# Two gate blocks by seven products of halves, and their layer's gate modulation moved to a later stage

## The chip, the cores and the metric

The kernel runs on one core of a Trainium2 chip. The metric is the device time of one execution in microseconds, as the median of several runs. The engines are TensorE (PE, its weight loads are listed as PEld), VectorE (DVE), ScalarE (ACT), GpSimd (POOL) and SyncE (SP). SP does no arithmetic here; it issues nearly all loads. POOL issues the stores to DRAM scratch.

## The reference

A trunk of two layers on 512 tokens of width 2048. Layer 1 is multi-scale retention, layer 2 multi-head latent attention with 16 heads. Each layer also has a SiLU gate path, and a modulation by a conditioning vector `c`:

```python
c_act = jax.nn.silu(c)
for i in range(DEPTH):
    mod = (c_act @ ada_w[i] + ada_b[i])[:, None, :]
    shift, scale, gate = jnp.split(mod, 3, axis=-1)
    h = rmsnorm(x, norm_g[i]) * (1.0 + scale) + shift
    y = branch(h)
    x = x + gate * y
return rmsnorm(x, final_norm_g)
```

and in the attention branch:

```python
proj = h @ w_in
cq, ckv, k_rope, g = jnp.split(proj, [512, 1024, 1088], axis=-1)
q = rmsnorm(cq, q_norm_g) @ w_uq
kv = rmsnorm(ckv, kv_norm_g) @ w_ukv
o = causal_block_attention(q, k, v)
return (jax.nn.silu(g) * o) @ w_out
```

The change concerns two things of layer 2: columns 1024 to 2047 of `g` (the third and fourth block of 512), and the third section of `mod`, the vector `gate` of 2048 values, which is first needed when the output projection is added to the residual.

## The kernel before

**Numbers.** Every operand of a large product is split in two parts: `hi` is the value rounded to the matmul's 32-bit type (ACT casts it), `lo` the rest (DVE subtracts). A product is three matmuls, hi·hi, hi·lo and lo·hi (`mm3`, lines 160 to 163). The activations of layer 2, `h2`, lie in SBUF as 16 tiles of 128 rows by 512 tokens in both parts.

**Two ways to multiply.** `plain_steps` (L727) walks through eight units of two 128-row tiles; a unit is 24 matmuls of 128x512 (two tiles, four column blocks, three parts). The other way halves both the columns of the weights and the tokens, and forms seven products of halves instead of eight, as in Strassen's scheme with Winograd's sums. It needs sums of halves of the activations, formed once (`form_sums`, L447, 16 tiles of `sums2` for layer 2), and sums of halves of the weights, formed by DVE for each unit. `seven_steps` (L795) does so for products whose result has tokens on its rows, among them the latents `cq` and `ckv`. `seven_rows_steps` (L876) does it for products with tokens along the free axis; layer 1's `q` and `k` of four heads use it. A block is eight steps: in the first phase four units of four products (48 matmuls of 128x256), in the second four units of three products (36 matmuls). Its four accumulators x, s, z, y are four PSUM banks of the tag `acc`.

**Order of layer 2.** The main loop takes a list of `steps`, each with its loads, a preparation (splits and sums of weights), its matmuls and what is hung beside it. Gate block 0 and 1 come first, then the latents, then gate blocks 2 and 3 (the list `g23`, 16 steps by `g2_steps`, L1613), and nine attention steps (`attention_step`, L1983), each of which projects two heads and attends the two before. The Silu of each gate block is stored in DRAM (`sg2_d`) and read back per head (`sg`). While `g23` runs, the latents are normed, transposed on PE and split into `k4` tiles. The last two heads are attended in hooks of the output projection, which has two runs of eight units (`o2_unit`, 24 matmuls of 128x512 each) and a last part of its own. `o2_parts` loads the attention's result (`o_in`) and splits it into `o_h` and `o_l`; `o2_unit` loads and splits `o_w`. In `o2_out` (L2192 to 2210) the gate vector multiplies the result.

**The gate's modulation.** `later_modulation` (L1061) loads the modulation's rows in pieces of 512 KB (`mod`) and DVE sums each against `silu(c)` with one instruction (L1078). The pieces of layer 2's gate, 32 of them, are requested by the argument `rows=2` of the 16 steps of `g23`: two loads a step, each summed one step later. Their buffers are `bw` (two) and `pt` (four); `silu(c)` lies in two `k4b` tiles.

**Order on the engines.** The program is emitted through a scheduler that may reorder instructions on an engine by their priority. `behind(engines)` holds what follows behind the last instruction already emitted on those engines; `queued(fn)` does so for ACT, DVE, PE and SP. Each engine then runs its instructions strictly in the resulting order, and a waiting instruction holds up everything behind it. Buffers are rings: a tile of a tag with two buffers waits until the last user of the tile before the last is done.

**Buffers of the sums.** `sums_tile(n)` (L443) puts sums tiles 0 to 7 into the eight `k4` buffers, 8 to 11 into `k4b`, 12 to 15 into `pt`. Unit `u` of the scheme reads tile `2u` in its first phase (`i = 0`) and `2u + 1` in its second.

Of the kernel before, what the change touches and what calls it, by code (L numbers as in the profile page):

```python
# [9 lines left out]
F32 = mybir.dt.float32  # L10
# [39 lines left out]
def hybrid_trunk_kernel(  # L50
# [44 lines left out]
    def big(name, dt=F32R):  # L95
        return base.tile([P, 2, T], dt, tag="big", bufs=16, name=name)
# [7 lines left out]
    def tmp(name, shape=(P, T)):  # L104
        return base.tile(list(shape), F32, tag="tmp", bufs=6, name=name)
# [325 lines left out]
    def queued(fn, *args):  # L431
        with behind(A_, V_, T_, S_):
            return fn(*args)
# [5 lines left out]
    def sums_tile(n, more):  # L439
        shape = [P, 2, 2, H]  # L440
        if n < 8:
            return base.tile(shape, F32R, tag="k4", bufs=8, name=f"sums_{n}")
        if n < 12:  # L443
            return base.tile(shape, F32R, tag="k4b", bufs=4, name=f"sums_{n}")
        return more(shape, f"sums_{n}")

    def form_sums(u, acts, sums, staged, more, late=False):  # L447
        e, o = (tmp(f"h_{2 * u + i}_f") for i in range(2))
        for f, kt in ((e, 2 * u), (o, 2 * u + 1)):
            DVE.tensor_add(f, acts[kt][:, 0, :].bitcast(F32), acts[kt][:, 1, :].bitcast(F32))  # L450
        f = staged(f"sums_{u}_f")
        DVE.tensor_add(f[0][:, 0, :], e[:, H:], o[:, H:])
        DVE.tensor_sub(f[0][:, 1, :], f[0][:, 0, :], e[:, :H])
        DVE.tensor_sub(f[1][:, 0, :], e[:, :H], e[:, H:])
        DVE.tensor_sub(f[1][:, 1, :], o[:, :H], f[0][:, 1, :])

        def part():
            for i in range(2):
                s = sums[2 * u + i] = sums_tile(2 * u + i, more)
                split(f[i], s[:, :, 0, :], s[:, :, 1, :])  # L460

        if late:
            return part
        part()
# [1148 lines left out]
    def g2_steps(gi, **kw):  # L1613
        def evac(b, ps):
            sgs = l2_tile("sg", 3, f"sgs_{gi}_{b}")
            ACT.activation(sgs, ps, AF.Silu)
            r0 = (gi * 4 + b) * P
            POOL.dma_start(sg2_d[r0 : r0 + P, :], sgs)

        return plain_steps(  # L1620
            8, 2, lambda u: [(whole, rows(w_mla_in, u, 2, 1088 + gi * 512, 512))], 512, f"g2_{gi}", acc, 4,
            lambda w, ki, kt, b: w_block(w, ki, b), lambda w, ki, kt, b: act_row(h2[kt]), evac, **kw,
        )
# [91 lines left out]
        return l2_tile("pt", 4, name, shape, F32R)  # L1715

    for u, step in enumerate((ga[5], ga[7], g1[0], g1[2], g1[3], g1[5], g1[6], g1[7])):
        step.beside["form"].append(lambda u=u: form_sums(u, h2, sums2, staged2, more2))

    latent = {}  # L1720

# [12 lines left out]
    def latent_norm(n):  # L1734
        if n == "q":
            DVE.tensor_scalar(out=qn_s, in0=qn_c, scalar1=192.0**-0.5, scalar2=None, op0=ALU.mult)
        ss = small(f"ss_{n}", NT)
        for t in range(NT):
            ACT.activation(tmp(f"{n}_sq{t}"), latent[n][t], AF.Square, accum_out=ss[:, t : t + 1])
        latent[n, "r"] = rsqrt(ss, NT, 1.0 / 512, f"{n}_r")  # L1740

    def latent_scale(n):
        for t in range(NT):
            r, v = latent[n, "r"][:, t : t + 1], latent[n][t]
            if t % 2:
                ACT.activation(v, v, AF.Identity, scale=r)
            else:
                DVE.tensor_scalar(out=v, in0=v, scalar1=r, scalar2=None, op0=ALU.mult)

    def latent_transposes(n):  # L1750
        latent[n, "ps"] = []
        for j in range(4):
            ps = aux(f"{n}T_{j}")
            for t in range(NT):
                PE.transpose(ps[:, t * P : (t + 1) * P], latent[n][t][:, j * P : (j + 1) * P], ident)
            latent[n, "ps"].append(ps)

    def latent_parts(n, g_c):
        latent[n, "T"] = []
        for j, ps in enumerate(latent[n, "ps"]):  # L1760
            dst = k4(f"{n}T_{j}")
            ACT.activation(dst[:, 0, :], ps, AF.Identity, scale=g_c[:, j : j + 1])
            DVE.scalar_tensor_tensor(
                out=dst[:, 1, :], in0=ps, scalar=g_c[:, j : j + 1], in1=dst[:, 0, :].bitcast(F32),
                op0=ALU.mult, op1=ALU.subtract,
            )
            latent[n, "T"].append(dst)
# [7 lines left out]
        "c", lambda kt, j: wc[kt * P : (kt + 1) * P, j, :], lambda n, u, b: form(h2, sums2, n, u, b), *turns2,  # L1775
        latent_rows, lambda second, u: 0,
    )
    g23 = g2_steps(2, rows=lambda u: 2) + g2_steps(3, rows=lambda u: 2)
    for i, n, g_c in ((0, "q", qn_s), (1, "kv", kvn_c)):
        g23[i].beside["form"].append(lambda n=n: latent_norm(n))  # L1780
        g23[i + 1].beside["form"].append(lambda n=n: latent_scale(n))
        g23[2 + 2 * i].beside["multiply"].append(lambda n=n: latent_transposes(n))
        g23[3 + 2 * i].beside["form"].append(lambda n=n, g_c=g_c: latent_parts(n, g_c))
    steps += g23


# [69 lines left out]
    def units_ahead():  # L1856
        with behind(S_):
            while unit_state[0] < min(unit_state[1] + 3, len(unit_order)):
                unit_load(*unit_order[unit_state[0]])
                unit_state[0] += 1  # L1860
# [46 lines left out]
    def attend(h):  # L1907
# [72 lines left out]

        return scores, exps, lambda: (queued(reciprocals), queued(normalise)), transposes, split_pt, load_gate, values, result

    def attention_step(pr):  # L1983

        nx = pr + 1
        here = [attend(2 * pr + s) for s in range(2)] if pr >= 0 else ()
        both = heads2[nx] = {}
        units_ahead()
        if here:
            (sc0, ex0, no0, tr0, sp0, lg0, va0, re0), (sc1, ex1, no1, tr1, sp1, lg1, va1, re1) = here  # L1990
            queued(lg0)
            queued(lg1)
        low = next_unit("ukv")
        if here:
            for i in range(NT):
                queued(sc0, i)
            for i in range(NT):
                queued(ex0, i)
        low()
        if here:  # L2000
            no0()
        queued(uq_products, nx, 2)
        if here:
            for i in range(NT):
                queued(sc1, i)
            for i in range(NT):
                queued(ex1, i)
        t1 = queued(rope_own, both["uq", 2], f"qr_{nx}")
        low = next_unit("ukv") if here else lambda: None
        if here:  # L2010
            no1()
        low()
        for b in range(2):
            queued(uq_products, nx, b)
        sw = queued(rope_swap, both["uq", 2], f"qr_{nx}")
        low = queued(part_pair, nx, "uq", 0)
        queued(rope_turn, t1, sw)
        queued(low)
        low = queued(part_pair, nx, "uq", 1)
        if here:  # L2020
            queued(tr0)
        queued(low)
        lows = [queued(sp0, j) for j in range(3)] if here else []
        both["qr"] = big(f"qr_{nx}")
        queued(rope_highs, t1, both["qr"])
        for low in lows:
            queued(low)
        queued(rope_lows, t1, both["qr"])
        for b in range(2):
            queued(uk_products, nx, b)  # L2030
            low = queued(part_pair, nx, "uk", b)
            low_w = next_unit("uq")
            queued(low)
            low_w()
        if here:
            queued(va0)
            queued(re0)
            queued(tr1)
            for low in [queued(sp1, j) for j in range(3)]:
                queued(low)  # L2040
        for j in range(2):
            queued(uv_products, nx, j)
            queued(queued(part_values, nx, j))
        if here:
            queued(va1)
            queued(re1)
# [12 lines left out]
    def all_rows():  # L2059
        pieces = [(0, 2, 0), (0, 2, 1), (1, 0, 0)]  # L2060
        yield from later_modulation(pieces, load_c(lpp, "bm", 2), lpp, [("bw", 2)])
        while "l1" not in pools:
            yield None
        l1p = pools["l1"]
        pieces = [(1, 0, 1), (1, 1, 0), (1, 1, 1)]
        yield from later_modulation(pieces, load_c(l1p, "odd1", 2), l1p, [("odd0", 2)])
        while "l2" not in pools:
            yield None
        yield from later_modulation(
            [(1, 2, n) for n in range(2)], load_c(base, "k4b", 4), pools["l2"], [("bw", 2), ("pt", 4), ("pt", 4)]  # L2070
        )

    later = all_rows()
    loads = [load for step in steps for load, _ in step.units]
# [93 lines left out]
    ss2 = l2p.tile([P, T], F32, tag="o2", bufs=2, name="x2_ss")  # L2168
    o2_in, o2_res = {}, {}

    def o2_hooks(i):
        l2_hooks.get(i, lambda: None)()

    def o2_parts(r, u):
        if u not in o2_in:
# [223 lines left out]
```

## Time and profile before

| | us |
|---|---|
| median of 3 runs | 2168.11 (2167.63 to 2168.21) |
| the profiled execution | 2168.69 |
| its span in the trace | 2166.9 |

The span in layer 2, read from the trace:

| stage | from, us | to, us |
|---|---|---|
| gate block 1 | 1475 | 1554 |
| latents by seven products | 1554 | 1631 |
| gate blocks 2 and 3, plain | 1631 | 1722 |
| attention steps | 1722 | 1963 |
| last heads and the projection's first two runs | 1963 | 2050 |
| last part of the projection and the end | 2050 | 2167 |

Gate block 1's row includes the forming of sums and the rotary key beside it. A row of a timeline gives start, duration, engine, line, operation, destination and sources, and in brackets how long the engine stood idle before it and what ended that. "MATMUL ... x48" is a group; a matmul's duration is longer than the distance of two starts, since they are pipelined. A row of stretches gives start and end, length, and for each engine its busy time with the number of instructions in brackets, then the granted clock of TensorE, the share of the DMA engines and GB/s.

### The profile page before, as it was taken

The numbers are of one execution on the slowest core, as the hardware profiler recorded it, in microseconds if no ns is written. First come the engines' busy times: TensorE is split into PE (matmuls) and PEld (weight loads), VectorE is DVE, ScalarE is ACT, GpSimd is POOL, SyncE is SP. The second block draws the span as 40 slices with busy tenths as digits, with TensorE's granted clock in tenths as the row PEclk, the third lists the DMA queues.
The fourth block names the chain that finished last, engine by engine and source line by source line (L and its number), as shares of the span: only waits on it lengthen the run. The fifth ranks groups of instructions, "written<-read, shape, count | busy, mean of one in ns | idle before, by whom it ended". The sixth has DMA issues, their size and how long they took to land.

```text
span 2166.9 us, 29190 instructions
## 1 busy us (share of the span) xinstructions
PE 2138.3 (99%) x10796; PEld 1817.2 (84%) x10796; DVE 1637.7 (76%) x2426; ACT 1038.9 (48%) x1580; POOL 106.1 (5%) x178
## 2 busy tenths in 40 slices
PE   8899999999999999999999999999999999999998
PEld 6788898988889888888888888888888889888887
DVE  7898788788878789766777777667977677775545
ACT  5674444444444444434344444445444365664444
POOL 1001000000000000000000000010001000000000
PEclk9999999999999999999999999999999999999999
DMA  9975687877777778765646557553458623335333
GB/s 382 381 282 192 222 272 233 270 243 257 260 255 252 231 238 280 246 200 173 231 163 224 203 201 251 173 177 103 161 185 319 244 88 100 92 106 183 111 101 136
DMA packets 218753, 456.08 MB, mean 210 GB/s; under 512 B 20161, under 2 KB 69345, under 8 KB 214769
## 3 DMA queue, kind: packets, MB, share of 16 engines
q1 hardware_dynamic: 206400, 415.04, 57.2%
q0 software_dynamic: 11920, 38.91, 4.6%
q8 instruction: 84, 1.38, 0.3%
q14 instruction: 59, 0.48, 0.1%
q10 hardware_dynamic: 290, 0.27, 0.1%
HBM read 411.15 MB, written 43.00 MB: 210 GB/s over the span
## 4 chain that ended last, share of the span: by engine, by line
PE 85%; DVE 5%; issue 4%; DMA 3%; ACT 2%; POOL 1%; SPq 0%; POOLq 0%; DVEq 0%; ACTq 0%
PE o L1376 12%; PE o L2235 4%; PE y L796 2%; PE y L797 2%; PE s L796 2%; PE y L795 2%; PE s L797 2%; PE x L797 2%; PE x L796 2%; PE s L795 2%; PE x L795 2%; PE x_qk L894 2%; PE y_qk L894 2%; PE s_qk L894 2%; PE o L162 2%
## 5 line engine op out<-in xcount | busy, mean ns | idle before, releaser
L1376 PE MATMUL o<-o_h,o_whi 128*128 128x512 f32 (+1 forms) x496 | 192.3, 388 | 0.0
L1376 PE MATMUL o<-o_h,o_wlo 128*128 128x512 f32 (+1 forms) x496 | 191.5, 386 | 0.1
L1376 PE MATMUL o<-o_l,o_whi 128*128 128x512 f32 (+1 forms) x496 | 191.3, 386 | 0.0
L1376 PEld LDWEIGHTS o<-o_h,o_wlo 128*128 128x128 f32 x496 | 93.2, 188 | 19.3 <-DVE o_wlo L136 0.6
L1376 PEld LDWEIGHTS o<-o_l,o_whi 128*128 128x128 f32 x496 | 93.2, 188 | 18.3
L1376 PEld LDWEIGHTS o<-o_h,o_whi 128*128 128x128 f32 x496 | 93.2, 188 | 18.3
L136 DVE TENSOR_TENSOR o_wlo<-o_r,o_whi 128x1024 fp32r<-128x1024 f32 x61 | 74.6, 1224 | 44.2 <-ACT o_whi L135 44.2
L161 PE MATMUL g<-h,g_h 128*128 128x512 f32 x232 | 90.6, 391 | 0.3 <-ACT g_h L135 0.3
L162 PE MATMUL g<-h,g_h 128*128 128x512 f32 x232 | 90.3, 389 | 0.0
L163 PE MATMUL g<-h,g_l 128*128 128x512 f32 x232 | 89.8, 389 | 0.0
L161 PE MATMUL qk<-hT,qk_h 128*128 128x512 f32 x192 | 74.9, 390 | 0.0
L162 PE MATMUL qk<-hT,qk_h 128*128 128x512 f32 x192 | 74.7, 389 | 0.0
L356 DVE SCALAR_TENSOR_TENSOR aw<-aw,c_all 128x2048 f32<-128x2048 f32 (+1 forms) x35 | 72.9, 2103 | 0.9 <-DMA aw<-in_ada_t_dram 0.9
L135 ACT CAST o_whi<-o_r 128x1024 fp32r<-128x1024 f32 x61 | 63.5, 1051 | 21.0 <-PE o L1376 17.6
L163 PE MATMUL qk<-hT,qk_l 128*128 128x512 f32 x192 | 73.4, 389 | 0.0
L1078 DVE SCALAR_TENSOR_TENSOR mod<-mod,c_odd 128x1024 f32<-128x1024 f32 x48 | 58.1, 1221 | 18.5 <-DMA mod<-in_ada_t_dram 18.5
L136 DVE TENSOR_TENSOR o_w_lo<-o_w_raw,o_w_hi 128x1024 fp32r<-128x1024 f32 x32 | 39.0, 1221 | 36.7 <-ACT o_w_hi L135 36.7
L136 DVE TENSOR_TENSOR o_l<-o_in,o_h 128x1024 fp32r<-128x1024 f32 x24 | 29.3, 1223 | 42.8 <-ACT o_h L135 42.8
L1078 DVE SCALAR_TENSOR_TENSOR mod<-mod,c_bm 128x1024 f32<-128x1024 f32 x48 | 58.6, 1220 | 0.0
L2235 PE MATMUL o<-o_h,o_w_hi 128*128 128x512 f32 (+1 forms) x160 | 55.6, 348 | 0.0
L2235 PE MATMUL o<-o_l,o_w_hi 128*128 128x512 f32 (+1 forms) x160 | 55.5, 347 | 0.0
L2235 PE MATMUL o<-o_h,o_w_lo 128*128 128x512 f32 (+1 forms) x160 | 55.5, 347 | 0.0
(1435 smaller groups left out, 6637.6 us busy)
## 6 DMA issues: line engine op xcount, KB each, us to landing
mod<-in_ada_t_dram SPq DMA_DIRECT2D x128, 512.0 KB, 6.2
o_r<-in_ret_w_out_dram SPq DMA_DIRECT2D x64, 512.0 KB, 5.4
aw<-in_ada_t_dram SPq DMA_DIRECT2D x30, 1024.0 KB, 9.9
g_r<-in_mla_w_in_dram SPq DMA_DIRECT2D x32, 512.0 KB, 4.3
o_w_raw<-in_mla_w_out_dram SPq DMA_DIRECT2D x32, 512.0 KB, 3.8
qk_r<-in_ret_w_in_dram SPq DMA_DIRECT2D x48, 256.0 KB, 3.4
qk_r<-qk_d SPq DMA_DIRECT2D x32, 256.0 KB, 6.2
v_r<-v_d SPq DMA_DIRECT2D x32, 256.0 KB, 6.0
```

What stands on the lines that cost most here:

```text
L136: DVE.tensor_sub(lo, src, hi.bitcast(F32))
L161: PE.matmul(o, lhs[0], rhs[0], start=first and not seeded, stop=False, skip_group_check=seeded)
L162: PE.matmul(o, lhs[0], rhs[1], start=False, stop=False, skip_group_check=seeded)
L163: return PE.matmul(o, lhs[1], rhs[0], start=False, stop=last, skip_group_check=seeded)
L356: DVE.scalar_tensor_tensor(out=aw[:, cols], in0=aw[:, cols], scalar=1.0, in1=c_all[:, cols], op0=ALU.mult, op1=ALU.mult, accum_out=col[:, ...
L795: PE.matmul(banks[b], a[0], w[0], start=first, stop=False, skip_group_check=True)
L796: PE.matmul(banks[b], a[0], w[1], start=False, stop=False, skip_group_check=True)
L797: PE.matmul(banks[b], a[1], w[0], start=False, stop=True, skip_group_check=True)
L894: PE.matmul(o, w[wp][:, i, b * P : (b + 1) * P], a[ap], start=first and i + b + k == 0, stop=k == 2, skip_group_check=True,)
L1078: DVE.scalar_tensor_tensor(out=aw, in0=aw, scalar=1.0, in1=silu_c[j], op0=ALU.mult, op1=ALU.mult, accum_out=mc[:, j, b : b + 1],)
L1376: PE.matmul(o, w[i][:, ki, c0 + b * P : c0 + (b + 1) * P], a[j], start=first and i + j == 0, stop=last and i == 1, skip_group_check=True,)
L2235: PE.matmul(banks2[b][:, cols], w[0][i][:, 0, b * P : (b + 1) * P], o2_moving(w, u, cols)[j], start=u + i + j == 0, stop=u == KD - 1 and i ...
```

## The change

1. Layer 2's sums are laid out by phase: all tiles of the first phase in `k4`, those of the second in `k4b` and `pt`.
2. Gate blocks 2 and 3 go through `seven_rows_steps` instead of `plain_steps`. A first-phase unit has four loads of 256 KB, a second-phase unit three, in place of one load of 512 KB.
3. The work on the latents beside them moves: q's from steps 0, 1, 2, 3 to 0, 4, 10, 11; kv's from 1, 2, 4, 5 to 1, 5, 12, 13.
4. The 32 loads and sums of the gate's modulation leave these blocks. The first 16 go two per attention step, the second 16 into hooks 4 to 14 of the output projection (one or two each, summed at the next hook). All use the two `bw` buffers; `silu(c)` is loaded anew for each half of eight, in tiles of the tag `big`.

```diff
-    def form_sums(u, acts, sums, staged, more, late=False):
+    def form_sums(u, acts, sums, staged, more, late=False, apart=False):
...
-                s = sums[2 * u + i] = sums_tile(2 * u + i, more)
+                s = sums[2 * u + i] = sums_tile(u + 8 * i if apart else 2 * u + i, more)
...
-        step.beside["form"].append(lambda u=u: form_sums(u, h2, sums2, staged2, more2))
+        step.beside["form"].append(lambda u=u: form_sums(u, h2, sums2, staged2, more2, apart=True))
...
-    g23 = g2_steps(2, rows=lambda u: 2) + g2_steps(3, rows=lambda u: 2)
-    for i, n, g_c in ((0, "q", qn_s), (1, "kv", kvn_c)):
-        g23[i].beside["form"].append(lambda n=n: latent_norm(n))
-        g23[i + 1].beside["form"].append(lambda n=n: latent_scale(n))
-        g23[2 + 2 * i].beside["multiply"].append(lambda n=n: latent_transposes(n))
-        g23[3 + 2 * i].beside["form"].append(lambda n=n, g_c=g_c: latent_parts(n, g_c))
+    def g2_seven(gi):
+        def load_half(u, odd_, j):
+            c0 = 1088 + gi * T + j * H
+            return w_mla_in[:, c0 : c0 + H].rearrange("(u i e p) n -> u e p i n", i=2, e=2, p=P)[u, odd_]
+        def finish(x, s, y, m4, m5):
+            def store(j, half, t):
+                r0 = (gi * 4 + 2 * j) * P
+                POOL.dma_start(
+                    sg2_d[r0 : r0 + 2 * P, half * H : (half + 1) * H].rearrange("(b p) n -> p b n", p=P),
+                    t.rearrange("p (b n) -> p b n", b=2),
+                )
+            for j, ps in enumerate((x, s)):
+                st = tmp(f"sgs_{gi}_{j}")
+                ACT.activation(st, ps, AF.Silu)
+                store(j, 0, st)
+            for j, m in enumerate((m4, m5)):
+                DVE.tensor_add(m, m, y)
+                ACT.activation(m, m, AF.Silu)
+                store(j, 1, m)
+        return seven_rows_steps(f"g2{gi}", load_half, h2, sums2, *turns2, finish, lambda second, u: 0)
+    g23 = g2_seven(2) + g2_seven(3)
+    for n, g_c, at in (("q", qn_s, (0, 4, 10, 11)), ("kv", kvn_c, (1, 5, 12, 13))):
+        g23[at[0]].beside["form"].append(lambda n=n: latent_norm(n))
+        g23[at[1]].beside["form"].append(lambda n=n: latent_scale(n))
+        g23[at[2]].beside["multiply"].append(lambda n=n: latent_transposes(n))
+        g23[at[3]].beside["form"].append(lambda n=n, g_c=g_c: latent_parts(n, g_c))
...
+    gate_c_half = {}
+    gate_sums = [base.tile([P, 2, 8], F32, tag="mod_c", bufs=2, name=f"gate_sums{i}") for i in range(2)]
+    def gate_load(part, n):
+        j, b = n // 8, n % 8
+        if b == 0:
+            half = gate_c_half[j] = big(f"c_gate{part}{j}", F32)
+            nc.sync.dma_start(
+                half.rearrange("p a n -> p (a n)"),
+                c_d[0:1, j * 1024 : (j + 1) * 1024].rearrange("o n -> (o n)").partition_broadcast(P),
+            )
+        aw = l2_tile("bw", 2, f"mod_gate_{part}{b}{j}", (P, 2, T))
+        r0 = 2 * D + (8 * part + b) * P
+        nc.sync.dma_start(aw, ada_t[1, r0 : r0 + P, j * 1024 : (j + 1) * 1024].rearrange("p (a n) -> p a n", a=2))
+        return aw, part, j, b, gate_c_half[j]
+    def gate_sum(aw, part, j, b, c_half):
+        DVE.scalar_tensor_tensor(
+            out=aw, in0=aw, scalar=1.0, in1=c_half, op0=ALU.mult, op1=ALU.mult,
+            accum_out=gate_sums[part][:, j, b : b + 1],
+        )
+        if (j, b) == (1, 7):
+            use_modulation(1, 2, part, gate_sums[part])
...
         units_ahead()
+        with behind(S_):
+            sums = [gate_load(0, 2 * nx + i) for i in range(2)]
...
             queued(uv_products, nx, j)
+            queued(gate_sum, *sums[j])
             queued(queued(part_values, nx, j))
...
-        while "l2" not in pools:
-            yield None
-        yield from later_modulation(
-            [(1, 2, n) for n in range(2)], load_c(base, "k4b", 4), pools["l2"], [("bw", 2), ("pt", 4), ("pt", 4)]
-        )
...
+    gate_pending, gate_n = [], [0, 0]
     def o2_hooks(i):
         l2_hooks.get(i, lambda: None)()
+        while gate_pending:
+            gate_sum(*gate_pending.pop())
+        for _ in range(1 + i % 2 if 3 < i < 15 and i > gate_n[1] else 0):
+            gate_pending.insert(0, gate_load(1, gate_n[0]))
+            gate_n[0] += 1
+        gate_n[1] = i
```

In the order that results, the first two loads of the output projection's share stand on SP between the gate values of the last head (`sg`) and the first `o_in`. On DVE its first sum stands among the last head's reductions, and from the fourth unit on two sums stand before each unit's `o_l` and the next unit's `o_w_lo`.

## The prediction

> **What bounds the kernel now.** I read the page from the top: the share of each engine and the clock, then the chain that ended last.
>
> ```profile
> PE 2138.3 (99%) x10796; PEld 1817.2 (84%) x10796; DVE 1637.7 (76%) x2426; ACT 1038.9 (48%) x1580; POOL 106.1 (5%) x178
> ...
> PEclk9999999999999999999999999999999999999999
> ...
> PE 85%; DVE 5%; issue 4%; DMA 3%; ACT 2%; POOL 1%; SPq 0%; POOLq 0%; DVEq 0%; ACTq 0%
> ```
>
> TensorE is busy 99% of the span at full clock and is 85% of the chain. A change can gain only by taking work off PE, and lose only by making PE wait. So the next view is what PE waits for, as totals by line (us, times, longest): the first row below is one of the large ones, from layer 1; the other two are the only ones from the stages touched here.
>
> ```profile
> PE qk L407 <- ACT qk L394: 3.1, 1, 3.1
> ...
> PE g L161 <- ACT g_h L135: 0.3, 1, 0.3
> ...
> PE a L161 <- ACT p L1933: 0.2, 1, 0.2
> ```
>
> Then the busy time by stretches of time. In order: a layer-1 stage that already uses seven products of halves, the layer-2 latents that do too, gate blocks two and three, attention, the last two heads with the start of the output projection, and its steady part.
>
> ```profile
> 283.00:329.00 46.00, 46.00 (x362) 44.83 (x361) 39.79 (x51) 23.20 (x29) 5.15 (x10) 1.00 0.82 279
> ...
> 1554.00:1630.00 76.00, 75.90 (x331) 61.54 (x330) 55.16 (x66) 35.96 (x45) 2.15 (x4) 1.00 0.58 190
> 1630.00:1676.00 46.00, 46.00 (x221) 38.48 (x220) 37.56 (x61) 21.45 (x40) 4.30 (x3) 1.00 0.89 328
> 1676.00:1722.00 46.00, 46.00 (x205) 38.09 (x204) 28.21 (x41) 13.39 (x18) 3.06 (x7) 1.00 0.76 278
> ...
> 1752.00:1962.00 210.00, 210.00 (x1276) 189.07 (x1276) 157.49 (x308) 132.07 (x288) 7.02 (x13) 1.00 0.32 100
> 1962.00:2000.00 38.00, 37.82 (x200) 32.55 (x199) 22.30 (x41) 19.14 (x37) 1.62 (x3) 1.00 0.54 185
> 2000.00:2040.00 40.00, 40.00 (x178) 33.14 (x177) 22.89 (x23) 19.17 (x23) 0.00 (x0) 1.00 0.40 126
> ```
>
> The columns are length, PE, weight load, DVE, ACT, POOL, clock, DMA share, GB/s. PE fills every one of these stretches. The gate blocks are where DMA is fullest (0.89), the attention where it is emptiest (0.32).
>
> **The products (a gain).** Two blocks of 512 columns take 2 x 8 units of 24 matmuls, 384 of 128x512. By halves each block takes 4 units of 48 and 4 of 36 matmuls of 128x256, 672 for both. What one costs is the distance of starts, not its duration, since they overlap. For 512 columns I read it from ACT's casts of the gate weights, which PE releases once a unit; for 256 columns from the first start of each unit of the layer-1 seven-product stage.
>
> ```profile
> 1694.76 1.06 ACT L135 CAST g_h<-g_r 128x1024 fp32r<-128x1024 f32 x1 [4.38 <-PE g L162]
> 1700.20 1.05 ACT L135 CAST g_h<-g_r 128x1024 fp32r<-128x1024 f32 x1 [4.38 <-PE g L162]
> ```
>
> ```profile
> L894 PE MATMUL x_qk<-hT,qk_00e_h x32: 280/283/283, 289.0 to 642.5; 128*128 128x256 f32 x32
> L894 PE MATMUL x_qk<-hT,qk_01e_h x32: 283/283/284, 294.8 to 648.3; 128*128 128x256 f32 x32
> ...
> L894 PE MATMUL x_qk<-hT,qk_10o_h x32: 280/282/283, 312.0 to 665.5; 128*128 128x256 f32 x32
> L894 PE MATMUL x_qk<-hT,qk_11o_h x32: 283/283/284, 316.3 to 669.8; 128*128 128x256 f32 x32
> ```
>
> 5.44 / 24 = 0.2267 us; 5.8 / 48 and 4.3 / 36 give 0.120 us. So 384 x 0.2267 = 87.05 us become 672 x 0.120 = 80.6 us: **-6.5 us**. Counting multiplications alone (seven for eight) would promise an eighth, 10.9 us; the 256-column matmul keeps 0.0067 us over half a 512-column one, and that eats 4.4 us. The Trainium skill ("TensorE: Matmul & The Clock Gate", section "Wait — 56ns, not 53.3ns?") puts the distance at columns over 2.4 GHz plus about 2.5 ns; by it the gain would be 9.4 us, but this trace has 226.7 and 120 ns where the rule makes 215.7 and 109.2, so the rows decide.
>
> Can the other engines feed it? The two precedents answer: in the layer-1 stretch PE is busy 46.00 of 46.00 with DVE at 39.79, in the latents 75.90 of 76.00 with the same buffers as here. Loads grow from 4 to 7 MB a block in pieces of 256 KB, but 32 loads of 512 KB for the modulation leave, so the stretch's DMA share must fall from 0.89 / 0.76 toward the latents' 0.58. Silu and stores stay at four a block; two DVE sums a block are new. The latents' norm, transposes and parts issue the same instructions up to eleven units later, the last parts two units before the stage ends, so the attention's first products do not wait. I take 0 for all this, between 0 and +2 us (a late bank at each of two block starts, at most a cast's 1.06 us each).
>
> **The modulation beside attention (nothing).** What is moved are 32 loads and 32 sums, and the row of the sums and of the loads in the old place are:
>
> ```profile
> L1078 DVE SCALAR_TENSOR_TENSOR mod<-mod,c_k4b x32: 1214/1222/1226, 1634.5 to 1722.7; 128x1024 f32<-128x1024 f32 x32
> ...
> mod<-in_ada_t_dram SPq DMA_DIRECT2D x32, 512.0 KB, 7.3
> ```
>
> Sixteen go two per attention step, each on DVE right after the issue of the V products and ahead of the low part of `v`. There DVE waits anyway:
>
> ```profile
> L1793 DVE TENSOR_TENSOR v<-uv,v 128x512 fp32r<-128x512 f32 x15 | 10.3, 691 | 25.8 <-ACT v L1792 25.8
> ```
>
> 25.8 / 15 = 1.7 us idle before each, against 1.22 us. DVE goes from 157.49 of 210 to about 175. On SP the two loads precede the gate values of the heads; they wait until the sums of the step before have freed their two buffers, and the units' weight loads stand behind them, with some 5 us to spare of a step of 29. If the cover were gone, it would be 16 x 1.2 = 19 us; nothing in the row suggests that.
>
> **The start of the output projection (a loss).** Sixteen sums stand in the output projection. Their first two loads are issued on SP ahead of the attention outputs that the projection reads (`o_in`). Each needs a buffer freed by one of the last two sums of the attention. Now SP does this:
>
> ```profile
> 1956.28 0.34 SPq L1964 DMA_DIRECT2D sg<-sg_d  x1
> 1957.09 13.93 SPq L2177 DMA_DIRECT2D o_in<-o_d  x7
> ```
>
> DVE and ACT around it, and PE behind them:
>
> ```profile
> 1956.16 1.62 DVE L1793 TENSOR_TENSOR pt<-pT,pt 128x512 fp32r<-128x512 f32 x3
> 1959.68 0.69 DVE L1793 TENSOR_TENSOR v<-uv,v 128x512 fp32r<-128x512 f32 x1 [1.90 <-ACT v L1792]
> ```
>
> ```profile
> 1963.57 1.05 ACT L135 CAST o_h<-o_in 128x1024 fp32r<-128x1024 f32 x1 [1.04 <-DMA o_in<-o_d]
> ...
> 1965.78 0.47 ACT L1933 ACTIVATE p<-a,nb 128x256 f32<-128x256 f32 x1 [0.28 <-DVE nb L1932]
> ```
>
> ```profile
> 1967.33 0.33 PE L161 MATMUL a<-ukT,uqT 128*128 128x256 f32 x1
> ...
> 1968.54 0.44 PE L161 MATMUL a<-ukT,uqT 128*128 128x384 f32 x1 [0.18 <-ACT p L1933]
> ```
>
> The next-to-last sum follows `pt` (1957.8) and ends near 1959.0; the last follows `v` (1960.4) and ends near 1961.6. SP then issues the second modulation load and comes to `o_in` near 1962.0 instead of 1957.09, 5 us late. Landing took until 1963.57, 6.4 us; so `o_h` can begin at 1968.4 and ends at 1969.4. In ACT's order it stands in front of the second exponential (0.47 us), which ends near 1969.9 and frees the scores' bank that PE takes at 1967.33: a stall of 2.5 us, and 0.6 more for the next cast between the third and fourth exponential. **+3.1 us.** Bounds: this transfer's eight landings are in its view by tile.
>
> ```profile
> L135 ACT CAST o_h<-o_in x24: 1037/1050/1055, 1963.6 to 2118.0; 128x1024 fp32r<-128x1024 f32 x24
> ...
> DMA to landing us min/median/max: 3.5/7.3/11.5
> ```
>
> At 3.5 us the stall is gone; at 11.5 it is 7.6 us. I take the 6.4 of the first transfer itself. A broadcast load of `silu(c)` behind the `o_in` holds the first of these sums, and three reductions of the last head queue behind it on DVE; they have about 1.6 us to spare, which I count as none.
>
> **The sums in the projection's units (a small loss).** From there DVE has per unit of 5.44 us two sums, `o_l`, and the next `o_w_lo`: 4 x 1.14 = 4.6 us, where it now is idle before each `o_l`.
>
> ```profile
> 2004.82 1.23 DVE L136 TENSOR_TENSOR o_l<-o_in,o_h 128x1024 fp32r<-128x1024 f32 x1 [3.08 <-ACT o_h L135]
> 2005.96 1.22 DVE L136 TENSOR_TENSOR o_w_lo<-o_w_raw,o_w_hi 128x1024 fp32r<-128x1024 f32 x1
> 2010.26 1.22 DVE L136 TENSOR_TENSOR o_l<-o_in,o_h 128x1024 fp32r<-128x1024 f32 x1 [3.08 <-ACT o_h L135]
> ```
>
> It fits if the loads arrive in time, and that is the open point: with two buffers a load is issued only when the sum before last is done, so a pair takes landing + 1.2 us. At the weights' landing in this stage, 3.8 us (row below), that is 5.0 and fits into 5.44; at the 7.3 us the same loads took in the gate blocks it is 8.5. `o_l` has about 3.1 us of slack before PE needs it: `o_h` is cast when a unit begins, 5.44 - 1.05 - 1.23 = 3.1.
>
> ```profile
> o_w_raw<-in_mla_w_out_dram SPq DMA_DIRECT2D x32, 512.0 KB, 3.8
> ```
>
> The stretch's DMA share is 0.40, so I lean to 3.8, with one longer landing: **+0.5 us** (0 to 11). The rest to the end is unchanged.
>
> **Sum.** -6.5 + 3.1 + 0.5 = -2.9 us. The profiled execution took 2168.69 us (span 2166.9 and 1.8 around it), so it would take 2165.8; it lies 0.58 above the median of 2168.11, so the median becomes **2165.2 us**.
>
> **Rivals.** *B, the start does not stall:* the `o_in` land in 3.5 us in a queue that their lateness has emptied. For it: the share around is 0.54. Against: the first one took 6.4. Time 2168.1 - 6.5 = 2161.6.
> *C, the two buffers set the pace (slower):* in the projection each pair of sums takes 8.5 us against 5.44, over about five pairs 15.3, less 3.1 to 4 of slack, 11 us; it decides once the landing exceeds 4.2 us (5.44 - 1.2). For it: the load's own row, 7.3, and that `o_in` and weights queue on the same SP. Against: DMA 0.40. Time 2168.1 - 6.5 + 3.1 + 11 = 2175.7, and more if the stall at the start passes 3 us, since a long wait also costs clock here: PE was idle for 3.1 us in the first stretch below, and the next ran at 0.66, 1.4 us lost (length, PE, clock, DMA share, GB/s).
>
> ```profile
> 76.00:80.00 4.00, 0.94 (x5) 0.92 1.04 421
> 80.00:84.00 4.00, 4.00 (x12) 0.66 1.00 406
> ```
>
> The Trainium skill (same page, section "HAM oscillation — how this bites in real kernels") has an idle window of about 3.4 us for this; the trace agrees in kind at 3.1.
> *D, half the columns cost half the time here:* 672 x 0.1133 = 76.2 us, a gain of 10.9 instead of 6.5; with the same stalls 2160.8. The skill's rule above points this way. Against: every unit of the layer-1 rows shows 0.120.
>
> **How the numbers follow.** A (the sum) 0.42, own range 2163 to 2168; B 0.35; C 0.18; D 0.05. About 0.2% (4.3 us, below 2163.8 or above 2172.4) is what a measurement of this kernel tells from no change. Faster: B, D and the low end of A, 0.45; same: the rest of A and a mild C, 0.39; slower 0.16. The range 2160.5 to 2175.5 leaves out half of D, a tail of B and the upper half of C, 0.16 together.
>
> **What would show it.** Right: the new products' starts 0.120 apart with no PE wait in the stage; PE waits on `p` and `o_h` near the last head, 2 to 4 us together, behind an `o_in` issued 5 us later relative to the last gate values; DVE waiting on modulation loads in the projection, PE hardly. Wrong: PE waits at the gate blocks' banks or in attention steps, DVE's `v` later than PE's use of it, or a projection unit longer than 5.44 us.

## The result, and the profile after

The changed kernel takes 2171.8 us in the median of 20 runs (2167.46 to 2176.36), the kernel before 2168.2 us (2167.05 to 2170.25): a ratio of 1.0015, 95% interval 1.0009 to 1.0022. It is slower by about 3.6 us, where 2.9 us less were forecast. Its times also scatter almost three times as wide. The profiled execution took 2171.59 us, with a span of 2169.8.

The lines of the page that answer to those shown of before:

```profile
PE 2135.0 (98%) x11084; PEld 1828.2 (84%) x11084; DVE 1677.6 (77%) x2482; ACT 1055.9 (49%) x1602; POOL 106.8 (5%) x178
...
PEclk9999999999999999999999999999999999999999
```

PE has less work (2135.0 against 2138.3 us) in a longer span. So it waits. The view of PE's waits (total, times, longest) names two large ones in the stages of the change; the kernel before had 0.2 us on `p`, the exponentials of the scores, and none on `o_l`:

```profile
PE a L161 <- ACT p L1961: 4.3, 1, 4.3
...
PE o L162 <- DVE o_l L136: 2.6, 2, 1.5
```

To see where the time went I take three marks in the trace: the first and the last cast of `uqT` (attention) and the last product of the projection's second run with `o_w_lo`. First the rows of the kernel before, by tile (first and last start stand behind the durations), then the changed kernel's.

```profile
L1792 ACT CAST uqT<-uq x16: 577/588/597, 1729.2 to 1947.8; 128x512 fp32r<-128x512 f32 x16
...
L163 PE MATMUL o<-o_h,o_w_lo x128: 389/389/397, 1970.9 to 2063.4; 128*128 128x512 f32 x128
```

```profile
L1820 ACT CAST uqT<-uq x16: 577/588/597, 1721.5 to 1940.0; 128x512 fp32r<-128x512 f32 x16
...
L163 PE MATMUL o<-o_h,o_w_lo x128: 387/389/402, 1969.4 to 2065.6; 128*128 128x512 f32 x128
```

| distance, us | before | changed | difference |
|---|---|---|---|
| end of layer 1 (last `x_sums` of L1109, 1459.7 and 1458.2) to first `uqT` | 269.5 | 263.3 | -6.2 |
| first to last `uqT`: attention | 218.6 | 218.5 | -0.1 |
| last `uqT` to last `o_w_lo` of the second run | 115.6 | 125.6 | +10.0 |
| from there to the end of the span | 103.5 | 104.2 | +0.7 |

By these rows the projection's second run ends at 2063.4 in the kernel before; the 2050 of the table of stages is too early. The remaining -1.5 us lies in layer 1, which the change does not touch (over all ten profiles its end lies between 1458.2 and 1460.9). The products gain their 6.2 us, attention hides its sixteen sums, and the last heads with the projection's first two runs lose 10.0. The first mark is a cast on ACT. By PE's own first product of attention (`uq`, at 1722.0 and 1713.6) the products gain 6.9 us and attention is 0.6 longer, 0.4 in the kernel without the sums, so most of that is not theirs.

That the new products run as forecast is seen in the first starts of two units of the changed kernel, 5.7 us apart for 48 products, 0.119 us each; what attention still had to spare is the idle time of DVE before `v`, 10.1 us over 14 instructions where it was 25.8 over 15:

```profile
L894 PE MATMUL x_g<-h,g_00e_h x16: 279/282/287, 1629.8 to 1671.1; 128*128 128x256 f32 x16
L894 PE MATMUL x_g<-h,g_01e_h x16: 280/283/287, 1635.5 to 1676.9; 128*128 128x256 f32 x16
```

```profile
L1821 DVE TENSOR_TENSOR v<-uv,v 128x512 fp32r<-128x512 f32 x14 | 9.7, 691 | 10.2 <-ACT v L1820 10.1
```

The timelines of the place of the loss, changed kernel, first SP:

```profile
1948.45 0.34 SPq L1992 DMA_DIRECT2D sg<-sg_d  x1
1951.12 2.92 SPq L2027 DMA_DIRECT2D mod_gate<-in_ada_t_dram  x2
1954.21 2.83 SPq L2238 DMA_DIRECT2D o_in<-o_d  x4
```

then DVE's last two sums of the attention, ACT, and PE:

```profile
1949.87 1.21 DVE L2031 SCALAR_TENSOR_TENSOR mod_gate<-mod_gate,c_gate 128x1024 f32<-128x1024 f32 x1
...
1952.46 1.22 DVE L2031 SCALAR_TENSOR_TENSOR mod_gate<-mod_gate,c_gate 128x1024 f32<-128x1024 f32 x1
```

```profile
1962.35 1.04 ACT L135 CAST o_h<-o_in 128x1024 fp32r<-128x1024 f32 x1 [4.66 <-DMA o_in<-o_d]
1963.30 0.47 ACT L1961 ACTIVATE p<-a,nb 128x256 f32<-128x256 f32 x1
```

```profile
1963.91 0.58 PE L161 MATMUL a<-ukT,uqT 128*128 128x256 f32 x1 [4.25 <-ACT p L1961]
```

Read from bottom to top: PE waits 4.25 us for a scores bank (a PSUM buffer of the scores); ACT frees it with the exponential at 1963.30, which stands behind the cast of `o_h`; that cast waits 4.66 us for `o_in`, which SP issued at 1954.21, 5.8 us after `sg` (0.8 before); in between stand the two modulation loads, each released by one of DVE's two sums. What follows is seen in stretches of 2 us (length, PE, clock, DMA share, GB/s):

```profile
1964.00:1966.00 2.00, 2.00 (x8) 0.50 1.03 402
1966.00:1968.00 2.00, 2.00 (x6) 0.50 0.86 321
1968.00:1970.00 2.00, 2.00 (x8) 0.77 0.23 84
```

After the wait PE runs at half clock for some 5 us, about 2.5 us lost (2 x 0.5 + 2 x 0.5 + 2 x 0.23, an estimate from these rows). The Trainium skill ("TensorE: Matmul & The Clock Gate", section "HAM oscillation — how this bites in real kernels") says that an idle gap beyond about 3.4 us brings PE back to half clock; this wait of 4.25 us agrees.

The waits on `o_l` come later, in the projection's units. The first follows two sums, of which one waited for the broadcast of `silu(c)`; before the second DVE had no idle time from 2018.12 on, with sums, splits and the evacuations of the first run (DVE reads results out of PSUM) in turn. DVE, then PE:

```profile
2004.71 1.23 DVE L2031 SCALAR_TENSOR_TENSOR mod_gate<-mod_gate,c_gate 128x1024 f32<-128x1024 f32 x1 [4.50 <-DMA c_gate<-c_d]
```

```profile
2009.09 0.50 PE L162 MATMUL o<-o_l,o_w_hi 128*128 128x512 f32 x1 [1.04 <-DVE o_l L136]
...
2027.80 0.50 PE L162 MATMUL o<-o_l,o_w_hi 128*128 128x512 f32 x1 [1.52 <-DVE o_l L136]
```

### The profile page after: what moved, and what is told of

It reads as the page before. It is cut to its first block, busy times and chain, and to the rows that moved or that the text cites. A ratio compares the mean times of both kernels' runs of the same rounds, so it can differ in the third digit from the quotient of the medians.

```text
span 2169.8 us, 29982 instructions
## 1 busy us (share of the span) xinstructions
PE 2135.0 (98%) x11084; PEld 1828.2 (84%) x11084; DVE 1677.6 (77%) x2482; ACT 1055.9 (49%) x1602; POOL 106.8 (5%) x178
## 4 chain that ended last, share of the span: by engine, by line
PE 85%; DVE 4%; issue 4%; DMA 3%; ACT 2%; POOL 1%; SPq 0%; POOLq 0%; DVEq 0%; ACTq 0%
PE o L1376 13%; PE o L2296 4%; PE y L796 2%; PE y L797 2%; PE s L796 2%; PE y L795 2%; PE s L797 2%; PE x L797 2%; PE x L796 2%; PE s L795 2%; PE x L795 2%; PE x_qk L894 2%; PE y_qk L894 2%; PE s_qk L894 2%; PE qk L407 2%
## 5 line engine op out<-in xcount | busy, mean ns | idle before, releaser
L162 PE MATMUL o<-o_l,o_w_hi 128*128 128x512 f32 x128 | 50.5, 395 | 2.6 <-DVE o_l L136 2.6
L1231 ACT ACTIVATE yn<-y,nmr,gn_r 128x512 f32<-128x512 f32 x32 | 22.3, 778 | 62.0 <-DVE nmr L1225 62.0
L135 ACT CAST o_w_hi<-o_w_raw 128x1024 fp32r<-128x1024 f32 x32 | 33.5, 1051 | 38.7 <-PE o L2296 33.8
L407 PE MATMUL v<-v_whi,hT 128*128 128x512 f32 x128 | 44.0, 417 | 7.2 <-ACT hT L379 7.2
## 6 DMA issues: line engine op xcount, KB each, us to landing
aw<-in_ada_t_dram SPq DMA_DIRECT2D x30, 1024.0 KB, 10.1
```

Of the source, the lines that this page charges most:

```text
L135: ACT.copy(hi, src)
L162: PE.matmul(o, lhs[0], rhs[1], start=False, stop=False, skip_group_check=seeded)
L407: PE.matmul(banks[kind][b], lhs[i], rhs[j], start=kt == 0 and i + j == 0, stop=kt == KD - 1 and late, skip_group_check=True,)
```

## The experiments

Ratios are against runs of the kernel before on the same chip, whose medians were 2168.36 us for the first four, 2168.59 for the next two and 2169.53 for the last two. The fourth column is the third distance of the table above, from each kernel's profile; the last is from the view of PE's waits, in us. A profile is one execution: that of "cast behind exponentials" took 2.4 us less than its median, those of "loads behind" and "start only" 1.4 more, that of "move only" 1.3 less.

| kernel | median, us | ratio (95%) | last `uqT` to end of second run | PE's wait on p; on `o_l` |
|---|---|---|---|---|
| products only | 2162.69 | 0.9975 (0.9964 to 0.9985) | 115.7 | 0.2; none |
| move only | 2178.4 | 1.0045 (1.0033 to 1.0058) | 123.0 | 2.9; 2.1 |
| loads behind | 2164.02 | 0.9981 (0.9972 to 0.9990) | 116.8 | 0.6; 0.5 |
| cast behind exponentials | 2174.84 | 1.0029 (1.0019 to 1.0040) | 126.6 | see there; 2.0 |
| without the last pair | 2165.67, one run | | 119.2 | 1.5; 1.2 |
| late sums | 2163.07 | 0.9973 (0.9962 to 0.9983) | 115.6 | 0.2; none |
| start only | 2169.0 | 0.9999 (0.9990 to 1.0008) | 122.1 | 4.1; none |
| one broadcast | 2172.38 | 1.0015 (1.0005 to 1.0024) | 125.7 | 3.9; 3.1 |

**Products only.**

```diff
-        with behind(S_):
-            sums = [gate_load(0, 2 * nx + i) for i in range(2)]
...
-            queued(gate_sum, *sums[j])
...
-        for _ in range(1 + i % 2 if 3 < i < 15 and i > gate_n[1] else 0):
-            gate_pending.insert(0, gate_load(1, gate_n[0]))
+        if i == 4:
+            for part in range(2):
+                DVE.memset(gate_sums[part], 0.0)
+                use_modulation(1, 2, part, gate_sums[part])
+        for _ in ():
+            pass
             gate_n[0] += 1
```

> The seven products alone: no load and no sum of layer 2's gate modulation is left in the kernel, and the gate vector is the bias only (so the gate's product with c is left out of the result). Theory: the products save 6.2 us (the attention of the changed kernel begins 7.7 us earlier in its trace, 1.5 of which lie before the gate blocks), and everything lost came with the moved modulation: 2162.0 us against 2168.2, with no PE wait above 0.5 us after the gate blocks. Rival (the smaller matmuls or the block boundaries eat the gain): 2165 or more.

Measured: 2162.69 us, 5.7 less than the 2168.36 beside it, and the distance from the end of layer 1 to the first `uqT` is 263.3 us as in the changed kernel. The products do what the rows of layer 1 promised, and no wait of PE after them is above 0.3 us.

**Move only.** The kernel before with the modulation's functions and hooks of the change; `g2_steps` without its rows.

```diff
-    g23 = g2_steps(2, rows=lambda u: 2) + g2_steps(3, rows=lambda u: 2)
+    g23 = g2_steps(2) + g2_steps(3)
...
+        with behind(S_):
+            sums = [gate_load(0, 2 * nx + i) for i in range(2)]
...
+            queued(gate_sum, *sums[j])
```

> The kernel before, plain gate blocks, with only the modulation moved to attention and output projection as in the change. Theory: the loss is the move's own, about 10 us, in the last heads and the first two runs of the projection: 2178 us, with a PE wait of 3 to 5 us on p followed by a stretch at 0.6 to 0.7 clock. Rival (the loss comes from meeting the seven products' later stores of the gate path, so it needs both): 2169 to 2171.

Measured: 2178.4 us, 10.0 more, with the wait on p, and slow clock behind it. In the profile 7.4 of 8.4 us lie in the stretch of the fourth column. The rows are PE's waits and two stretches of this kernel:

```profile
PE a L161 <- ACT p L1933: 2.9, 1, 2.9
...
PE o L162 <- DVE o_l L136: 2.1, 3, 1.2
```

```profile
1973.00:1975.00 2.00, 2.00 (x7) 0.50 1.05 417
1975.00:1977.00 2.00, 2.00 (x8) 0.76 0.97 362
```

The loss needs no seven products; it belongs to the move. In this profile half clock followed a wait of 2.9 us. The Trainium skill ("TensorE: Matmul & The Clock Gate", section "HAM oscillation — how this bites in real kernels") speaks of 3.4 us; here the measurement decides.

**Loads behind.**

```diff
         for _ in range(1 + i % 2 if 3 < i < 15 and i > gate_n[1] else 0):
-            gate_pending.insert(0, gate_load(1, gate_n[0]))
+            with behind(S_):
+                gate_pending.insert(0, gate_load(1, gate_n[0]))
```

> The changed kernel with the projection's modulation loads held on SP behind the loads that stand before them in the program, so that o_in 0 to 3 are issued first; same loads, same buffers, same sums. Theory (o_in comes late because SP waits for the attention's last two sums before it can issue it): the start stall of 4.3 us and the slow clock behind it go, 6 us less: 2165.6 us. Rival (the bytes of the modulation and of the broadcast of silu(c) delay o_in, whatever the order): a wait of 2 to 4 us stays, 2169 to 2172.

Measured: 2164.02 us, 1.6 us better than the theory's figure. SP now issues `o_in` right behind `sg`, and PE's wait at the last head is 0.59 us:

```profile
1951.07 0.34 SPq L1992 DMA_DIRECT2D sg<-sg_d  x1
1951.51 3.09 SPq L2239 DMA_DIRECT2D o_in<-o_d  x4
1954.69 1.33 SPq L2021 DMA_DIRECT2D c_gate<-c_d  x1
```

```profile
1963.77 0.44 PE L161 MATMUL a<-ukT,uqT 128*128 128x384 f32 x1 [0.59 <-ACT p L1961]
```

The same loads and sums are still in the kernel, so the order on SP carries the start's loss. One line of code gives back nearly all of it. The edit holds all sixteen loads, not only the first two, and the waits on `o_l` fell with it, from 2.6 to 0.5 us. That agrees with a gain beyond the theory's 6 us. DVE's order of sums is another here (several stand alone where the changed kernel has pairs), so this run does not tell whether the loads' order or the sums' took the loss out of the units.

**Cast behind exponentials.** A hold on ACT for the first two casts, taken before the unit's weights are split.

```diff
-    def o2_parts(r, u):
+    def o2_parts(r, u, anchor=None):
...
-        split(o2_in[u], hi, lo)
+        if anchor is not None:
+            with tc.issue_after(anchor):
+                split(o2_in[u], hi, lo)
+        else:
+            split(o2_in[u], hi, lo)
...
     def o2_unit(r, u, kn, cn, where=None):
+        anchor = None
+        if r == 0 and u < 2:
+            anchor = next(i for i in reversed(nc.cur_bb.bb.instructions) if i.engine == A_)
...
-            o2_split[k] = o2_parts(*k)
+            o2_split[k] = o2_parts(*k, anchor)
```

> The changed kernel with its order on SP, but the casts o_h of the projection's first two units held on ACT behind the exponentials of the last head. Theory (the late o_in hurts since its cast stands in front of exponentials that free the scores' banks): PE goes on with scores and transposes until about the time o_in lands, the wait shrinks from 4.3 to about 1 us and the clock holds: 2166.5 us. Rival (the late load by itself sets the end, wherever its cast stands): the wait only moves to the first product of the projection, 2170 to 2172.

Measured: 2174.84 us; the theory missed. The exponentials no longer wait for `o_in` and PE runs through the scores, but a longer wait comes later. PE, and DVE at that place, in this kernel:

```profile
1963.68 1.45 PE L1983 MATMUL pT<-ident,p 128*128 128x128 f32 x10 [1.09 <-ACT p L1961]
...
1969.53 0.80 PE L162 MATMUL o<-pt,v 128*128 128x512 f32 x1 [3.19 <-DVE pt L1821]
```

```profile
1967.63 1.23 DVE L2031 SCALAR_TENSOR_TENSOR mod_gate<-mod_gate,c_gate 128x1024 f32<-128x1024 f32 x1 [3.33 <-DMA c_gate<-c_d]
1968.78 0.08 DVE L2031 DVE_READ_ACCUMULATOR mod_gate<-mod_gate,c_gate 128x1 f32 x1
1968.78 0.69 DVE L1821 TENSOR_TENSOR pt<-pT,pt 128x512 fp32r<-128x512 f32 x1
```

It is not the wait that the rival named either: PE now waits for `pt`, and on DVE `pt` stands behind the projection's first modulation sum, which waits 3.33 us for the broadcast of `silu(c)`. In the changed kernel DVE came to that sum only at 1969.78 and did not wait: the first delay had hidden a second, of the same kind on another engine.

**Without the last pair.** The last two pieces beside attention are left out of the sum; the projection's first two loads are then held on SP between `sg` and `o_in`, and their sums on DVE behind what stands before them.

```diff
-            sums = [gate_load(0, 2 * nx + i) for i in range(2)]
+            sums = [gate_load(0, 2 * nx + i) for i in range(2)] if nx < 7 else None
...
+    def ahead_of_o():
+        for n in range(2):
+            with behind(S_):
+                early.append(gate_load(1, n, 'rows'))
+        o_anchor.append(next(i for i in reversed(nc.cur_bb.bb.instructions) if i.engine == S_))
...
-            nc.sync.dma_start(o2_in[u], o2_d[u * 2 * P : (u + 1) * 2 * P, :].rearrange("(k p) n -> p k n", p=P))
+            with tc.issue_after(o_anchor[0]):
+                nc.sync.dma_start(o2_in[u], o2_d[u * 2 * P : (u + 1) * 2 * P, :].rearrange("(k p) n -> p k n", p=P))
```

> The changed kernel without the last two of the sixteen pieces beside attention (they are left out of the gate's sum), so that the two buffers are free long before; the projection's first two modulation loads still stand on SP ahead of o_in, and the broadcast of silu(c) behind o_in 3 as in the change. It tells the wait on SP from the bytes ahead of o_in. Theory (the wait): o_in 0 is issued within 2 us of the last sg instead of 5.8, and the PE wait on p at the last head falls from 4.3 to below 1 us, with the clock at 1.0 behind it. Rival (the bytes): o_in 0 lands 3 us later than in the kernel before, and a wait of 2 to 4 us stays. The later sums are bunched in fewer units here, so the whole time (2163 to 2168) does not decide.

Measured, SP, ACT and PE in turn:

```profile
1949.61 0.34 SPq L1992 DMA_DIRECT2D sg<-sg_d  x1
1949.99 0.92 SPq L2031 DMA_DIRECT2D mod_gate<-in_ada_t_dram  x2
1951.07 3.33 SPq L2263 DMA_DIRECT2D o_in<-o_d  x4
```

```profile
1959.56 1.05 ACT L135 CAST o_h<-o_in 128x1024 fp32r<-128x1024 f32 x1 [3.69 <-DMA o_in<-o_d]
```

```profile
1961.01 0.33 PE L161 MATMUL a<-ukT,uqT 128*128 128x128 f32 x1 [0.68 <-ACT p L1961]
...
1963.48 0.44 PE L161 MATMUL a<-ukT,uqT 128*128 128x384 f32 x1 [0.82 <-ACT p L1961]
```

Issued 1.5 us after `sg`, `o_in` landed after 8.5 us (6.5 in the kernel before), and PE waits 1.5 us in two pieces, without loss of clock. So SP's wait for the buffers was the larger part of the 4.25 us. That the bytes ahead of `o_in` lengthen its landing is not shown: in "move only", with the two loads ahead, the first `o_in` landed after 6.8 us, in "loads behind", with the two loads behind it, after 8.3, and in the two kernels with no modulation load near after 6.8 (products only) and 7.7 (late sums). This is one profile.

**Late sums.** The projection's sixteen loads and sums later: one load in each unit from the third of the second run on, held on SP.

```diff
-        for _ in range(1 + i % 2 if 3 < i < 15 and i > gate_n[1] else 0):
-            gate_pending.insert(0, gate_load(1, gate_n[0]))
+        if 9 < i < 26 and i > gate_n[1]:
+            with behind(S_):
+                gate_pending.insert(0, gate_load(1, gate_n[0]))
             gate_n[0] += 1
-        gate_n[1] = i
+            gate_n[1] = i
...
     for u in range(KD):
+        o2_hooks(16 + u)
         w = o2_unit(2, u, 1, ...)
```

> The changed kernel with the projection's sixteen loads and sums later: one in each unit from the third of its second run to the tenth of its last part (the second half of the gate vector is first used behind that), loads held on SP behind what stands before them. Theory (all that is left of the loss comes from loads and sums that meet the start of the projection and the end of its first run): no PE wait above 0.5 us after the gate blocks, 2162.0 to 2163.2, as with no modulation at all. Rival (a sum costs wherever it stands, through DVE's order or the weights' loads): 2164 or more.

Measured: 2163.07 us, ratio 0.9973, with all sums in place and no PE wait over 0.3 us after the gate blocks. It is level with the kernel without any modulation (0.9975) and beats both the kernel before and the changed one. DVE waits 10.5 us for modulation loads in its trace, and the view of PE's waits after the gate blocks names none for DVE.

**Start only.** The start of the change, then the late sums; the edit is shown against the kernel with the late sums.

```diff
+        if i in (4, 5) and i > gate_n[1]:
+            gate_pending.insert(0, gate_load(1, gate_n[0]))
+            gate_n[0] += 1
+            gate_n[1] = i
-        if 9 < i < 26 and i > gate_n[1]:
+        if 11 < i < 26 and i > gate_n[1]:
```

> The changed kernel's start of the output projection as it is (two modulation loads on SP ahead of o_in, the broadcast of silu(c) behind o_in 3, the same order on DVE and ACT), and the other fourteen loads and sums late, one a unit from the fifth unit of the second run on. It prices the start alone; what the change costs above it is the price of the sums in the first run's units. Theory: the start is the greater part, 6 to 7 us with its slow clock, so 2168.5 to 2170 against 2163 without it, and no PE wait on o_l. Rival (most of the loss is in the units, by o_l waits and what they leave behind): 2165 to 2167.

Measured: 2169.0 us, level with the kernel before beside it (2169.53). The distance to the end of the second run is 122.1 us, 6.5 more than before, and there is no wait on `o_l`; by ratios, 0.9999 against 0.9973 of the late sums, it is 5.6 us. The start thus costs 5.6 to 6.5 us. What is left for the sums in the units is 3.5 us, both by the profiles (10.0 less 6.5) and by the ratios (1.0015 less 0.9999).

**One broadcast.**

```diff
-        if b == 0:
+        if b == 0 and (part, j) != (1, 1):
             half = gate_c_half[j] = big(f"c_gate{part}{j}", F32)
...
-        return aw, part, j, b, gate_c_half[j]
+        return aw, part, j, b, gate_c_half[0 if part else j]
```

> The changed kernel with the second broadcast of silu(c) in the projection left out: the last eight pieces are summed against the first half of silu(c), so the second half of the gate vector is another number. It splits the two PE waits on o_l (1.0 and 1.5 us in the changed kernel's trace). Theory: the first is DVE waiting 4.5 us for that broadcast in front of o_l and goes; the second is DVE having more work than a unit holds at the end of the first run, with the sums among its evacuations, and stays at 1 to 2 us. Time 1 us less than the change, 2170 to 2171.5. Rival (both are the two buffers' loop): both stay.

Measured: 2172.38 us, the change's own ratio; the waits on `o_l` add up to 3.1 us. In the changed kernel DVE had waited 4.50 us for the broadcast in front of one sum. Without it DVE waits for the sums' own loads instead, two of these rows of DVE here:

```profile
2000.03 1.23 DVE L2031 SCALAR_TENSOR_TENSOR mod_gate<-mod_gate,c_gate 128x1024 f32<-128x1024 f32 x1 [3.30 <-DMA mod_gate<-in_ada_t_dram]
...
2018.14 1.23 DVE L2031 SCALAR_TENSOR_TENSOR mod_gate<-mod_gate,c_gate 128x1024 f32<-128x1024 f32 x1 [2.29 <-DMA mod_gate<-in_ada_t_dram]
```

```profile
2021.85 0.50 PE L162 MATMUL o<-o_l,o_w_hi 128*128 128x512 f32 x1 [1.35 <-DVE o_l L136]
2029.11 0.50 PE L162 MATMUL o<-o_l,o_w_hi 128*128 128x512 f32 x1 [1.50 <-DVE o_l L136]
```

The theory's first half fell: no broadcast is needed for the loss in the units. Its second half and the rival are not told apart by this run: the wait at 2021.85 follows a late load, and before the one at 2029.11 DVE had no idle time from 2018.14 on, with evacuations and sums in turn. The changed kernel's own trace has the same two forms, and no run takes them apart.

## Why the prediction was wrong, point by point

**Products, -6.5 us:** right. -6.2 us between the marks, 263.3 us to the first `uqT` in the changed kernel and in the one with the products only; the interval of 0.120 us for 256 columns held, and PE's waits name nothing above 0.3 us at the blocks' boundaries. The prediction's own figures give 6.4 (87.05 less 672 x 0.120). Rival D, a gain of 10.9, is out with it.

**Beside attention, 0 us:** right. The stretch is 218.5 against 218.6 us, and 218.3 with the products only; DVE still has idle time before `v`.

**Start of the output projection, +3.1 us: this step failed, in its size.** Its mechanism, its place and its order were right: "SP then issues the second modulation load and comes to `o_in` near 1962.0 instead of 1957.09, 5 us late". On the scale of the kernel before, 1954.21 is 1962.0 (7.8 us earlier in this stretch). Even the rule of the wait held: in four kernels PE waited 3.9 us less than the first `o_in` took to land, as the forecast's 2.5 for 6.4 has it.

| kernel | landing of the first `o_in`, us | PE's wait on p, us | difference |
|---|---|---|---|
| changed | 8.14 | 4.25 | 3.89 |
| move only | 6.84 | 2.94 | 3.90 |
| start only | 8.04 | 4.14 | 3.90 |
| one broadcast | 7.82 | 3.92 | 3.90 |

Two terms were mis-sized. The landing was taken from one transfer, 6.4 us, and was 8.1; what lengthens it is open, since it lies between 6.5 and 8.5 us over the nine profiles in which the first cast waits for it, with and without modulation loads near. And the price of a lost clock, worked out to 1.4 us, was put into a rival alone, for a start whose stall "passes 3 us", where the forecast's own bounds of the stall already reached 7.6: it cost about 2.5 us. The 0.6 us for a second cast did not come; PE waits on `p` once. That makes some 6.7 us in the changed kernel's trace, against the 6.5 of the profile and the 5.6 by ratios of the kernel with the start alone.

**Sums in the projection's units, +0.5 us: this step failed, in its size.** It measured 3.5 us (10.0 less 6.5). The projection's modulation loads had a median landing of 5.1 us (4.6 over all 32), between the 3.8 taken and the 7.3 of rival C, and longer than the 4.2 us at which the prediction itself had the two buffers set the pace. But the late sums have 5.2 and lose nothing, so the landing alone is not the cause. The prediction also counted four DVE instructions a unit throughout and left out the evacuations at the end of the first run, where the longer of the two waits on `o_l` lies (1.52 us, the other 1.04). Which of the two cost more is open, and so is the rest of the 3.5 us.

**The rivals.** B (no stall at the start) is out. C had the right sign and the right two places, but put 11 us into the units and 3.1 into the start; the greater part lay in the start. The forecast's sign went wrong since two losses, both foreseen, were each taken near the low end of their bounds: 3.1 + 0.5 against 6.5 + 3.5. That the median of 2171.8 us stayed inside the range stated is owed to the range's width, not to the sum.

The scatter of the changed kernel, 8.9 us against 3.2, agrees with a start that hangs on when one transfer lands; that was not tried by itself.

## What to carry to other kernels

A prefetch that waits for a buffer holds up every load behind it on its queue; ask first when that buffer comes free, and what stands behind. Where a stall is priced, take the landing time as a range over several transfers and not as one value, and put the clock that may be lost behind a stall of 2 us or more into the forecast itself. Work that is needed only at the end goes late, to where the engine and the queue have idle time: the same sixteen sums cost 10 us at the projection's start and in its first units and nothing measurable later.

## What was not expected of the hardware

The length of a wait does not decide by itself whether the clock falls. In "move only" a wait of 2.9 us was followed by about 4 us at half to three quarters of the clock; waits of 0.6 to 0.8 us, in "loads behind" and "without the last pair", left it at 1.00. The start of the kernel, which no change touches, has both cases between these. In the kernel before, a wait of 1.81 us was followed by 0.59 over 4 us, and one of 2.85 us by 1.00 (length, PE, clock, DMA share, GB/s in the second and fourth row):

```profile
23.69 0.50 PE L407 MATMUL v<-v_whi,hT 128*128 128x512 f32 x1 [1.81 <-ACT hT L379]
24.00:28.00 4.00, 4.00 (x12) 0.59 1.00 388
```

```profile
67.36 0.50 PE L407 MATMUL v<-v_whi,hT 128*128 128x512 f32 x1 [2.85 <-ACT hT L379]
68.00:72.00 4.00, 3.42 (x15) 1.00 1.03 420
```

In the changed kernel the same wait, 2.86 us, was followed by 0.61:

```profile
67.41 0.57 PE L407 MATMUL v<-v_whi,hT 128*128 128x512 f32 x1 [2.86 <-ACT hT L379]
68.00:72.00 4.00, 4.00 (x12) 0.61 1.03 418
```

The broadcast of `silu(c)`, 512 KB to all partitions, took 11.1 us to land at the crowded start of the projection and 5.4 us later on in the same kernel; a queue's median would have hidden that.
